# An encoder layer on one core: sums of weights and a product moved from GpSimd to VectorE, and the residual of the down projection added later

## The chip, the cores and the metric

The kernel runs on one core of a Trainium2 chip. A core has TensorE (PE in the rows), with its weight loads counted apart (PEld), VectorE (DVE), ScalarE (ACT), GpSimd (POOL) and SyncE (SP), which issues most DMAs. The metric is the device time of one execution in microseconds (us), the median of three runs; smaller is better.

## The reference

One layer of an encoder over 1024 + 256 tokens of width 1024: neighbourhood attention beside a short convolution, an output projection, a LayerNorm, then a gated feed-forward block. All is float32. The change touches the second half:

```python
x = layer_norm(DEEPNORM_ALPHA * x + mix, ln1_g, ln1_b)
h = dwconv3(x @ ffn_w_up + ffn_b_up, ffn_conv_w, ffn_conv_b)   # 1024 -> 5632
h_gate, h_val = jnp.split(h, 2, axis=-1)
f = (jax.nn.gelu(h_gate) * h_val) @ ffn_w_down + ffn_b_down    # 2816 -> 1024
return layer_norm(DEEPNORM_ALPHA * x + f, ln2_g, ln2_b)
```

## The kernel before

Each large product is done by Strassen's scheme in Winograd's form: seven products of half-size blocks in place of eight, with sums of the blocks before and after. Each block is split in a high part (a cast on ScalarE) and a low part (source less high part, on VectorE, line 69), and one product is three passes: high by high, low by high, high by low.

**The up projection** (class `Sevens`, lines 81 to 154; loop of line 1150) handles 22 pairs of 128-column tiles of the up weights: tile i of the gate with tile i of the value. A pair has four weight blocks a11, a12, a21, a22 (128x512 each, tile `ur`) and seven products in the order 1, 2, 6, 7, 4, 5, 3. Four sums of weight blocks are needed for a pair, and GpSimd makes them: line 112 (tile `us`), 113, 127 and 129. A slot n of the loop issues product n (24 matmuls of 128x320), then the split of the weights of product n + 2 (high part `uh`, low part `ul`, three buffers each, so the cast waits until product n - 1 has been read), then the eviction of product n - 1 (VectorE adds from PSUM, line 154), then what was put at that slot. At a pair's first product, four slots ahead, stand lines 112 and 113 (`sums_a`). After a pair's last product come its two convolutions (ScalarE line 997, VectorE lines 1000 to 1007), GELU on ScalarE (line 1012), the product of gate and value on GpSimd (line 1013), and its store (line 1014). Products of pairs 0 and 1 are interleaved, and beside them VectorE makes the seven forms of the activations (`xh`, `xl`).

**The down projection** (line 1374) runs seven products in the order 1, 7, 5, 6, 4, 2, 3, each of 11 steps; a step q is 15 matmuls of 128x512 (five token tiles t by three passes) into five of eight PSUM banks, and `dn_next` prepares the operands (`wd`, `fd`, `hr`) of a step some steps ahead. A product of the next kind starts on three free banks and then takes the first banks of the product before it, so these must be evicted by then. `at_step(q, f)` runs f after step q's matmuls are issued. The residual rows (x after the first LayerNorm, scaled by `gr` and shifted by `br`, lines 1214 and 1215) are loaded and scaled that way. Block c11 of product 1 is added by VectorE to the residual that already lies in `y` (line 1239), after ScalarE has copied the same bank into c12 (line 1237).

Each engine runs its instructions in the order in which the program issues them, so a waiting instruction holds up all that stands behind it on its engine.

Of the kernel before, what the change touches and what calls it, by code (L numbers as in the profile page):

```python
# [13 lines left out]
ALU = mybir.AluOpType  # L14
# [4 lines left out]
D = 1024  # L19
# [5 lines left out]
FFT = 22  # L25
# [14 lines left out]
def encoder_kernel(ctx: ExitStack, tc: tile.TileContext, a: dict, y_prompt, y_sample):  # L40
    nc = tc.nc

    def pool(name, side="left", bufs=1, space=None):
        kw = {} if space is None else {"space": space}
        if space is None:
            kw["side"] = side
        return tc.alloc_tile_pool(name=name, bufs=bufs, reuse_waits="tile", **kw)
# [23 lines left out]
    def split2(hi, lo, src):  # L71
        nc.scalar.copy(hi, src)  # L72
        diff(lo, src, hi.bitcast(F32))
# [7 lines left out]
    class Sevens:  # L81


        def __init__(self, seq, st, xops, uw, src, raw_tile, sum_tile, c_tile):
            self.seq, self.st, self.xops, self.uw, self.src = seq, st, xops, uw, src
            self.raw_tile, self.sum_tile, self.c_tile = raw_tile, sum_tile, c_tile
            self.pos = {ip: n for n, ip in enumerate(seq)}
            self.pairs = 1 + max(i for i, _ in seq)
            self.raws, self.sums, self.wops, self.slots, self.c, self.later = {}, {}, {}, {}, ({}, {}), {}
            self.done = set()  # L90
# [17 lines left out]
        def sums_a(self, i):  # L108
            if i < self.pairs:
                a11, a12, a21, a22 = self.blocks(i)  # L110
                self.sums[i] = self.sum_tile(i)
                nc.gpsimd.tensor_tensor(self.sums[i], a21, a22, ALU.add)  # L112
                nc.gpsimd.tensor_tensor(a21, a11, a21, ALU.subtract)

        def weights(self, n):
            if n >= len(self.seq) or n in self.done:
                return
            self.done.add(n)
            i, p = self.seq[n]
            a11, a12, a21, a22 = self.blocks(i)  # L120
            src = {1: a11, 2: a12, 6: a11, 7: a21, 4: a22, 5: self.sums.get(i), 3: a22}[p]
            wh, wl = self.wops[n] = [self.uw.tile([P, 512], F32R, tag=tag, name=tag, bufs=3) for tag in ("uh", "ul")]
            split2(wh, wl, src)
            if p == 1:
                if i not in self.sums:
                    self.sums_a(i)
                nc.gpsimd.tensor_tensor(a11, self.sums[i], a11, ALU.subtract)  # L127
            if p == 4:
                nc.gpsimd.tensor_tensor(a22, a12, a11, ALU.subtract)  # L129
                self.load(i + 2, 0)  # L130
            if p == 3:
                self.load(i + 2, 1)
# [29 lines left out]
    uw = pool("uw")  # L162
# [9 lines left out]
    def pair_of(p, pl):  # L172
        return [p.tile([P, 4, HALF], F32R, name=f"x{part}{pl}") for part in "hl"]

    xops = {p: pair_of(xqa, p) for p in (3, 2, 6)}
# [5 lines left out]
    def up_tile(tag, dt=F32):  # L181
        return up.tile([P, T], dt, tag=tag, name=tag, bufs={"c0": 2, "c1": 1, "o": 3, "wr": 2}[tag])
# [5 lines left out]
    def xblock(k, h):  # L188
        return xr[k][:, h * HALF:(h + 1) * HALF].rearrange("p (t c) -> p t c", c=P)
# [24 lines left out]
    def v_mm(ps, t, k):  # L214
# [8 lines left out]
    seq = [(i, p) for i in range(NPAIR) for p in ORDER]  # L223
    st = []
    pr7 = Sevens(seq, st, xops, uw, lambda i, g: a["w_in"][TILES[i][g]],
                 lambda i, g: uw.tile([P, 1024], F32, tag=f"ur{g}", name="ur", bufs=2),
                 lambda i: uw.tile([P, 512], F32, tag="us", name="us"),
                 lambda i, g: up_tile(f"c{g}"))

    v_dram = dram.tile([NT, P, 512], F32, name="v_dram")  # L230
    ps = {t: pa.tile([P, 512], F32, tag="pa", name="ps_v") for t in range(8)}
# [161 lines left out]
    for p, n in ((7, 0), (4, 1), (5, 2)):  # L393
        for k in range(4):
            src = {7: xblock(k, 0), 4: xblock(k + 4, 0), 5: xblock(k, 1)}[p]
# [417 lines left out]
    def bank():  # L813
        return cc.tile([P, 512], F32, tag="cc", name="ps_ch")
# [39 lines left out]
    st = [pool("st0", bufs=2, space=PSUM)]  # L854
# [7 lines left out]
    x1_dram = dram.tile([NT, P, D], F32, name="x1_dram")  # L862
# [45 lines left out]
    xops = {}  # L908
# [15 lines left out]
    for t, half in [(0, 0), (1, 0), (0, 1), (1, 1)] + [(t, half) for t in range(2, NT) for half in range(2)]:  # L924
# [4 lines left out]
        if t < 2 and half == 0:  # L929
            ps = early[t]  # L930
        else:
            ps = big.tile([P, 512], F32, tag="big", name="ps_o")
# [39 lines left out]
    uw = pool("uw")  # L972
    seq = [(i, p) for p in ORDER for i in range(2)] + [(i, p) for i in range(2, FFT) for p in ORDER]
# [9 lines left out]
            return last_c  # L983
        return (uw, up)[g].tile([P, T], F32, tag="c", name="c", bufs=2)

    up7 = Sevens(seq, st, xops, uw, lambda i, g: a["w_up"][i + g * FFT], raw_tile, sum_tile, c_tile)
    pos, NS = up7.pos, len(seq)
    c1, c2 = up7.c
    at_slot, run_slot = up7.at_slot, up7.run_slot
# [20 lines left out]

    def gated(i, o, u):
        nc.scalar.activation(o, o, AF.Gelu_apprx_tanh)  # L1012
        nc.gpsimd.tensor_tensor(o, o, u, ALU.mult)  # L1013
        nc.sync.dma_start(out=h_dram[i], in_=o)

    def value_conv(i, e):
# [18 lines left out]
    for i in range(2, FFT):  # L1035
        at_slot(pos[i, 3], lambda i=i: value_conv(i, pos[i, 3] + 1))
        at_slot(pos[i, 1] - 4, lambda i=i: sums_a(i))
# [31 lines left out]
    a11, hraws, wraws, hs, ws, ahead = {}, {}, {}, {}, {}, [0, 0]  # L1069
# [143 lines left out]
    def residual(dst, c):
        nc.vector.tensor_tensor(dst, dst, gr[:, c], ALU.mult)
        nc.vector.tensor_tensor(dst, dst, br[:, c], ALU.add)

    def add(dst, p, q):
        nc.vector.tensor_tensor(dst, p, q, ALU.add)  # L1218

    def add_sum(t, half, q):  # L1220

        cs = (L, R)[half]
        if t < HT - 1 or t >= HT:
            nc.vector.tensor_tensor_reduce(out=ys[t][:, cs], in0=ys[t][:, cs], in1=q, scale=1.0, scalar=0.0,
                                           op0=ALU.add, op1=ALU.add, accum_out=ss[t][:, 6 + half:7 + half])
        else:
            add(ys[t][:, cs], ys[t][:, cs], q)
            nc.vector.bn_stats(stats[t][:, half, :], ys[t][:, cs])
# [5 lines left out]
    def dn_evict(p, t, ps):  # L1234
        (c11, c12), (c21, c22) = ((ys[u][:, L], ys[u][:, R]) for u in (t, t + HT))
        if p in (1, 7, 5):
            nc.scalar.copy({1: c12, 7: c21, 5: c22}[p], ps)
        if p == 1:
            add(c11, c11, ps)
        if p == 6:  # L1240
            add(c12, c12, ps)
        if p == 4:
            add_sum(t + HT, 0, ps)
        if p in (2, 3):
            add_sum(t, int(p == 3), ps)
# [4 lines left out]
    def at_step(n, f):  # L1250
        beside.setdefault(n, []).append(f)
# [9 lines left out]
        nc.vector.scalar_tensor_tensor(br, br, ALPHA, rest["bd"], ALU.mult, ALU.add)  # L1261

    def left_in(t):
        nc.sync.dma_start(out=ys[t][:, L], in_=x1_dram[t][:, L])

    def right_in(t):
        rest[t] = dnraw[:, 0:3, :].rearrange("p a b -> p (a b)")[:, t * 512:(t + 1) * 512]
        nc.sync.dma_start(out=rest[t], in_=x1_dram[t][:, R])

    def row_in(t):  # L1270
        rest[t] = z_tile("yr")
        nc.sync.dma_start(out=rest[t], in_=x1_dram[t])

    def sums(t, part):
        (c11, c12), (c21, c22) = ((ys[u][:, L], ys[u][:, R]) for u in (t, t + HT))
        if part == 0:
            add(c21, c21, c12)
            add(c12, c12, c22)
        elif part == 1:
            add(c22, c22, c21)  # L1280
            add(c21, c21, rest[t + HT][:, L])
            add_sum(t + HT, 1, rest[t + HT][:, R])
        else:
            add(c12, c12, rest[t])
# [11 lines left out]
            store(t, slice(0, D))  # L1296

    at_step(0, rows_in)
    at_step(4, rows_scaled)
    at_step(40, lambda: (row_load(g2, "ln2_g"), row_load(b2, "ln2_b")))  # L1300
    for t in range(HT):
        u = t + HT
        for n, f in ((2 + t, lambda t=t: left_in(t)), (6 + t, lambda t=t: residual(ys[t][:, L], L)),
                     (12 + 2 * t, lambda u=u: row_in(u)), (16 + 2 * t, lambda u=u: residual(rest[u], slice(0, D))),
                     (26 + 2 * t, lambda t=t: right_in(t)), (30 + 2 * t, lambda t=t: residual(rest[t], R)),
                     (44 + 2 * t, lambda t=t: sums(t, 0)), (45 + 2 * t, lambda t=t: sums(t, 1)),
                     (56 + 2 * t, lambda t=t: sums(t, 2)),
                     ((55, 58, 61, 66, 69)[t], lambda u=u: second_norm(u, 0)),
                     ((57, 60, 63, 68, 70)[t], lambda u=u: second_norm(u, 1))):
            at_step(n, f)  # L1310
# [63 lines left out]
    for n, p in enumerate(DORDER):  # L1374
        ps = [banks[(5 * n + t + 4) % 8] for t in range(HT)]
# [131 lines left out]
```

## Time and profile before

| | |
|---|---|
| median of 3 runs | 1706.35 us (1704.37 to 1706.86) |
| profiled execution | 1705.61 us, of which the span of the profile is 1703.8 us |
| PE busy | 1654.1 us (97%) |
| PEld busy | 1534.1 us (90%) |
| DVE busy | 1299.6 us (76%) |
| ACT busy | 688.9 us (40%) |
| POOL busy | 485.6 us (28%) |
| up projection, about | 852 to 1421 us of the span |
| down projection, about | 1421 to 1692 us of the span |

Busy is the time in which an engine has an instruction running; matmuls overlap one another, so the busy share of PE says that it has work, not that it runs at its peak. An instruction that is held while it runs (here on VectorE) counts as busy for that time. Times in the rows are from the start of the span.

### The profile page before, as it was taken

To read this page: it belongs to the slowest core of one execution; us is meant where nothing else is said; L and a number is where in the kernel's file an instruction comes from. 1 tells how busy PE (TensorE), PEld (TensorE's weight loads), DVE (VectorE), ACT (ScalarE), POOL (GpSimd) and SP (SyncE) were. 2 spreads that over 40 slices of the span, in tenths; PEclk is the share of its full clock that TensorE was granted. 3 is DMA by queue.
4 is the path that set the end of the run, shared out by engine and by line. 5 is a ranking of instruction groups with operands and counts; after the bars stand their busy time and mean duration, and the time that the engine had idled before them with its cause. 6 is when DMAs were issued, how large, how long until landed. Compare 5 with 4: busy or idle time off the path is not lost.

```text
span 1703.8 us, 26121 instructions
## 1 busy us (share of the span) xinstructions
PE 1654.1 (97%) x9907; PEld 1534.1 (90%) x9915; DVE 1299.6 (76%) x2003; ACT 688.9 (40%) x1117; POOL 485.6 (28%) x423
## 2 busy tenths in 40 slices
PE   9999999999999998999999999999999999999997
PEld 7999999999997887777888899999999998788885
DVE  7567777877766776864689888888888888884886
ACT  4433344434445775323354333333333334332254
POOL 1221221222125672600012233333233232001145
PEclk9999999999999999999999999999999999999999
DMA  6277543677777551432401121122122117967753
GB/s 226 87 232 252 184 161 118 229 256 279 261 270 243 190 172 69 143 136 74 156 18 54 68 81 57 65 81 71 58 75 81 53 44 254 343 221 216 226 182 136
DMA packets 85196, 260.87 MB, mean 153 GB/s; under 512 B 9168, under 2 KB 16080, under 8 KB 85072
## 3 DMA queue, kind: packets, MB, share of 16 engines
q1 hardware_dynamic: 71392, 206.26, 34.9%
q0 software_dynamic: 11376, 44.57, 8.3%
q10 hardware_dynamic: 2304, 8.39, 1.4%
q8 instruction: 78, 1.28, 0.3%
q14 instruction: 46, 0.38, 0.1%
HBM read 171.10 MB, written 88.08 MB: 152 GB/s over the span
## 4 chain that ended last, share of the span: by engine, by line
PE 50%; DVE 9%; DMA 4%; issue 3%; ACT 2%; POOL 1%; SPq 0%; ACTq 0%; POOLq 0%; DVEq 0%
PE ps_x L57 26%; PE ps_dn L57 12%; PE ps_o L57 4%; PE ps_ch L591 3%; PE o_ps L57 2%; DVE ul L69 2%; PE s_ps L57 1%; PE t_ps L648 1%; DMA y<-x_dram 1%; DVE o L1000 1%; DMA ga<-sg_dram 1%; DVE ml L69 1%; DVE xl L69 1%; DVE c L154 1%; PE ps_ch L57 1%
## 5 line engine op out<-in xcount | busy, mean ns | idle before, releaser
L57 PE MATMUL ps_x<-xh,ul 128*128 128x320 f32 x2240 | 695.6, 311 | 8.0 <-DVE ul L69 7.5
L57 PE MATMUL ps_x<-xh,uh 128*128 128x320 f32 x2240 | 693.2, 309 | 1.1 <-ACT yb L899 0.7
L57 PE MATMUL ps_x<-xl,uh 128*128 128x320 f32 x2240 | 693.2, 309 | 0.4 <-DVE xl L69 0.3
L57 PEld LDWEIGHTS ps_x<-xh,ul 128*128 128x128 f32 x2240 | 422.1, 188 | 14.4 <-DVE ul L69 14.4
L57 PEld LDWEIGHTS ps_x<-xh,uh 128*128 128x128 f32 x2240 | 422.2, 188 | 1.8 <-ACT yb L899 1.1
L57 PEld LDWEIGHTS ps_x<-xl,uh 128*128 128x128 f32 x2240 | 422.2, 188 | 1.2 <-DVE xl L69 1.1
L69 DVE TENSOR_TENSOR ul<-ur,uh 128x512 fp32r<-128x512 f32 x240 | 203.8, 850 | 96.4 <-ACT uh L72 96.4
L57 PE MATMUL ps_dn<-wd,fd 128*128 128x512 f32 x1155 | 265.6, 392 | 6.6 <-DVE y L1218 3.6
L57 PEld LDWEIGHTS ps_dn<-wd,fd 128*128 128x128 f32 x1155 | 218.3, 189 | 53.6 <-DVE y L1218 4.0
L72 ACT CAST uh<-ur 128x512 fp32r<-128x512 f32 x240 | 147.0, 615 | 230.9 <-PE ps_x L57 182.2
L154 DVE TENSOR_TENSOR c<-ps_x,c 128x640 f32<-128x640 f32 x275 | 220.6, 813 | 1.1 <-PE ps_x L57 0.9
L129 POOL TENSOR_TENSOR ur<-ur 128x512 f32<-128x512 f32 x40 | 56.5, 1413 | 516.2 <-DVE ul L69 516.2
L69 DVE TENSOR_TENSOR ul<-us,uh 128x512 fp32r<-128x512 f32 x38 | 72.0, 1894 | 44.1 <-ACT uh L72 44.1
L997 ACT ACTIVATE o<-c,vec 128x1280 f32<-128x1280 f32 x43 | 62.5, 1458 | 78.5 <-DVE c L154 78.5
L1013 POOL TENSOR_TENSOR o<-o 128x1280 f32<-128x1280 f32 x22 | 65.4, 2975 | 92.7 <-ACT o L1012 80.0
L1000 DVE SCALAR_TENSOR_TENSOR o<-c,vec,o 128x1023 f32<-128x1023 f32 x86 | 89.4, 1040 | 1.6 <-ACT o L997 1.6
L1001 DVE SCALAR_TENSOR_TENSOR o<-c,vec,o 128x1023 f32<-128x1023 f32 x86 | 77.9, 905 | 3.0
L635 POOL TENSOR_TENSOR sp<-sp,stat 128x384 f32<-128x384 f32 (+1 forms) x80 | 59.5, 746 | 68.3 <-DVE stat L634 45.3
L112 POOL TENSOR_TENSOR us<-ur 128x512 f32<-128x512 f32 x38 | 50.9, 1340 | 91.6 <-DVE ul L69 47.9
L1012 ACT ACTIVATE o<-o 128x1280 f32<-128x1280 f32 x22 | 28.0, 1274 | 119.9 <-DVE o L1007 119.9
L1098 POOL DMA_DIRECT2D wd<-wd_dram x55 | 29.7, 539 | 160.6 <-PE ps_dn L57 144.4
L127 POOL TENSOR_TENSOR ur<-us,ur 128x512 f32<-128x512 f32 x38 | 49.6, 1304 | 83.6 <-DVE ul L69 83.5
(232 smaller groups left out, 2443.6 us busy)
## 6 DMA issues: line engine op xcount, KB each, us to landing
wd_dram<-wd SPq DMA_DIRECT2D x55, 512.0 KB, 3.3
wd<-wd_dram POOLq DMA_DIRECT2D x55, 512.0 KB, 4.5
ur<-in_w_up SPq DMA_DIRECT2D x44, 512.0 KB, 3.5
ur<-in_w_in SPq DMA_DIRECT2D x36, 512.0 KB, 4.4
qk_dram<-o SPq DMA_DIRECT2D x48, 320.0 KB, 5.5
h_dram<-o SPq DMA_DIRECT2D x22, 640.0 KB, 2.9
hr<-h_dram SPq DMA_DIRECT2D x33, 320.0 KB, 4.2
sg_dram<-c SPq DMA_DIRECT2D x16, 640.0 KB, 4.2
```

The lines of the kernel that those rows point to most:

```text
L57: nc.tensor.matmul(out, lhsT=l, rhs=r, start=(first and i == 0), stop=(last and i == n - 1))
L69: nc.vector.tensor_tensor(dst, p, q, ALU.subtract)
L72: nc.scalar.copy(hi, src)
L112: nc.gpsimd.tensor_tensor(self.sums[i], a21, a22, ALU.add)
L129: nc.gpsimd.tensor_tensor(a22, a12, a11, ALU.subtract)
L154: nc.vector.tensor_tensor(d, ps, q, ALU.add)
L591: nc.tensor.matmul(ps[:, :cn], lhsT=l, rhs=r, start=(i == 0), stop=(i == len(ops) - 1))
L635: nc.gpsimd.tensor_tensor(sp[:, :nk], sp[:, :nk], st[:, 2:3].to_broadcast([P, nk]), ALU.mult)
L997: nc.scalar.activation(o, c, AF.Identity, bias=beff[:, f:f + 1], scale=cw[1][:, f:f + 1])
L1000: nc.vector.scalar_tensor_tensor(o[:, s + 1:s + n], c[:, s:s + n - 1], w0, o[:, s + 1:s + n], ALU.mult, ALU.add)
L1001: nc.vector.scalar_tensor_tensor(o[:, s:s + n - 1], c[:, s + 1:s + n], w2, o[:, s:s + n - 1], ALU.mult, ALU.add)
L1013: nc.gpsimd.tensor_tensor(o, o, u, ALU.mult)
```

## The change

The class `Sevens` gets the engine of its sums as an argument: GpSimd as before for the input projection, VectorE for the up projection. The product of gate and value goes to VectorE as well. In the down projection the eviction of product 1 is two copies by ScalarE; the left residual is loaded into a buffer of its own (`yl`, from the ring of five `z` buffers), scaled there and added to `y` by VectorE at steps of the second product. The steps at which rows are loaded and scaled move back: the scaling of `gr` and `br` from step 4 to 10, the left rows from steps 2 to 10 to steps 9 to 22, the rows of the lower half from steps 12 to 24 to steps 20 to 32, the right rows from steps 26 to 38 to steps 29 to 41.

```diff
@@ class Sevens
-                nc.gpsimd.tensor_tensor(self.sums[i], a21, a22, ALU.add)
-                nc.gpsimd.tensor_tensor(a21, a11, a21, ALU.subtract)
+                self.eng.tensor_tensor(self.sums[i], a21, a22, ALU.add)
+                self.eng.tensor_tensor(a21, a11, a21, ALU.subtract)
...
-                nc.gpsimd.tensor_tensor(a11, self.sums[i], a11, ALU.subtract)
+                self.eng.tensor_tensor(a11, self.sums[i], a11, ALU.subtract)
             if p == 4:
-                nc.gpsimd.tensor_tensor(a22, a12, a11, ALU.subtract)
+                self.eng.tensor_tensor(a22, a12, a11, ALU.subtract)
@@ pr7 = Sevens(...)
-                 lambda i, g: up_tile(f"c{g}"))
+                 lambda i, g: up_tile(f"c{g}"), nc.gpsimd)
@@ up7 = Sevens(...)
-    up7 = Sevens(seq, st, xops, uw, lambda i, g: a["w_up"][i + g * FFT], raw_tile, sum_tile, c_tile)
+    up7 = Sevens(seq, st, xops, uw, lambda i, g: a["w_up"][i + g * FFT], raw_tile, sum_tile, c_tile, nc.vector)
@@ def gated
-        nc.gpsimd.tensor_tensor(o, o, u, ALU.mult)
+        nc.vector.tensor_tensor(o, o, u, ALU.mult)
@@ def dn_evict
         if p == 1:
-            add(c11, c11, ps)
+            nc.scalar.copy(c11, ps)
@@ def left_in
-        nc.sync.dma_start(out=ys[t][:, L], in_=x1_dram[t][:, L])
+        rest["l", t] = z_tile("yl")[:, L]
+        nc.sync.dma_start(out=rest["l", t], in_=x1_dram[t][:, L])
@@ at_step
-    at_step(4, rows_scaled)
+    at_step(10, rows_scaled)
...
-        for n, f in ((2 + t, lambda t=t: left_in(t)), (6 + t, lambda t=t: residual(ys[t][:, L], L)),
...
+        for n, f in ((9 + 2 * t, lambda t=t: left_in(t)), (13 + 2 * t, lambda t=t: residual(rest["l", t], L)),
+                     (14 + 2 * t, lambda t=t: add(ys[t][:, L], ys[t][:, L], rest["l", t])),
```

On VectorE, where the first pairs are worked on (`xl_9303` is the low part of the last form of the activations, `ur` here the weights of pair 2 and `us` their sum):

```order
 L69 TENSOR_TENSOR ul<-ur,uh 128x512
 L154 TENSOR_TENSOR c<-ps_x_9272,c 128x640
+L112 TENSOR_TENSOR us<-ur 128x512
+L113 TENSOR_TENSOR ur<-ur 128x512
 L69 TENSOR_TENSOR xl_9303<-yb_7971,xh_9302 128x640 x2
 L69 TENSOR_TENSOR ul<-ur,uh 128x512
 L154 TENSOR_TENSOR c<-ps_x_9308,c 128x640 x2
 L69 TENSOR_TENSOR ul<-ur,uh 128x512
+L127 TENSOR_TENSOR ur<-us,ur 128x512
```

Two sums now stand between an eviction and the low parts of the activations, and a third behind the low part of pair 2's first product.

On VectorE, at the border of two pairs in the steady part (`o` is the gate after its convolution, the product with it is line 1013):

```order
 L1006 TENSOR_SCALAR o_9441<-o_9441,t_443 128x2
 L1007 TENSOR_SCALAR o_9441<-o_9441,nw_444 128x2
+L1013 TENSOR_TENSOR o_9441<-o_9441 128x1280
 L69 TENSOR_TENSOR ul<-us,uh 128x512
 L154 TENSOR_TENSOR c<-ps_x_9770,c 128x640
+L112 TENSOR_TENSOR us<-ur 128x512
+L113 TENSOR_TENSOR ur<-ur 128x512
 L69 TENSOR_TENSOR ul<-ur,uh 128x512
 L154 TENSOR_TENSOR c<-ps_x_9810,c 128x640
 L69 TENSOR_TENSOR ul<-ur,uh 128x512
+L127 TENSOR_TENSOR ur<-us,ur 128x512
```

The product of line 1013, which takes the result of GELU, stands directly behind the last step of the convolution and ahead of the low part of the pair's product 5 (`us`).

On VectorE, at the change from the up to the down projection, behind the convolution of the last pair (`wd` and `fd` are operands of the down projection's step 4):

```order
 L1006 TENSOR_SCALAR o<-o,t_443 128x2
 L1007 TENSOR_SCALAR o<-o,nw_444 128x2
+L1013 TENSOR_TENSOR o<-o 128x1280
 L69 TENSOR_TENSOR wd<-hr,wd 128x512
 L69 TENSOR_TENSOR fd<-a_4_14232,fd 128x640
```

The last product of gate and value stands ahead of the operands of step 4.

## Rows read from the trace of the kernel before

**Rows 1.** Stretches: length, busy us by engine (instructions), clock, DMA share, GB/s

```profile
900.00:945.00 45.00, 38.70 (x253) 37.65 (x252) 41.08 (x51) 15.69 (x18) 16.55 (x9) 0.97 0.23 77
988.00:1013.00 25.00, 24.97 (x171) 24.70 (x170) 21.58 (x27) 8.69 (x11) 8.54 (x6) 1.00 0.20 69
1431.00:1442.00 11.00, 9.47 (x41) 7.47 (x41) 10.35 (x15) 6.80 (x11) 3.56 (x2) 1.00 0.63 193
1464.00:1471.00 7.00, 5.17 (x12) 4.11 (x13) 6.97 (x11) 3.11 (x6) 0.53 (x1) 0.52 0.95 334
1471.00:1500.00 29.00, 29.00 (x129) 23.95 (x129) 23.59 (x30) 8.66 (x14) 1.58 (x3) 1.00 0.85 285
```

**Rows 2.** Waits of PE: who waits for whom, us in total, times, longest

```profile
PE ps_x L57 <- DVE ul L69: 7.5, 6, 2.8
PE ps_dn L57 <- DVE y L1218: 3.6, 1, 3.6
```

**Rows 3.** Timeline, borders of pairs: start, us, engine, instruction [idle before <-releaser]

```profile
964.60 0.42 PE L57 MATMUL ps_x<-xh,ul 128*128 128x320 f32 x1 [1.09 <-DVE ul L69]
...
1059.11 0.22 DVE L1007 TENSOR_SCALAR o<-o,nw 128x2 f32<-128x2 f32 x1
1059.43 1.27 ACT L1012 ACTIVATE o<-o 128x1280 f32<-128x1280 f32 x1 [5.40 <-DVE o L1007]
1060.78 2.97 POOL L1013 TENSOR_TENSOR o<-o 128x1280 f32<-128x1280 f32 x1 [2.64 <-ACT o L1012]
1061.24 3.05 DVE L69 TENSOR_TENSOR ul<-us,uh 128x512 fp32r<-128x512 f32 x1 [1.91 <-ACT uh L72]
1064.01 0.31 PE L57 MATMUL ps_x<-xl,uh 128*128 128x320 f32 x1
1064.35 0.41 PE L57 MATMUL ps_x<-xh,ul 128*128 128x320 f32 x1
```

**Rows 4.** Groups by form, DVE from 965 to 1364 us: count, busy, mean ns, idle before

```profile
L69 DVE TENSOR_TENSOR ul<-ur,uh 128x512 fp32r<-128x512 f32 x96 | 91.3, 951 | 20.8 <-ACT uh L72 20.8
L69 DVE TENSOR_TENSOR ul<-us,uh 128x512 fp32r<-128x512 f32 x16 | 48.8, 3051 | 30.8 <-ACT uh L72 30.8
```

**Rows 5.** Groups by form, DVE from 850 us on

```profile
L1214 DVE TENSOR_TENSOR y<-y,dnraw 128x512 f32<-128x512 f32 x5 | 3.4, 689 | 1.0 <-DMA y<-x_dram 1.0
```

**Rows 6.** Timeline, first pairs of the up projection

```profile
892.97 1.35 ACT L72 CAST xh<-yb 128x640 fp32r<-128x640 f32 x2 [4.10 <-POOL ur L129]
...
902.15 1.55 DVE L69 TENSOR_TENSOR xl<-yb,xh 128x640 fp32r<-128x640 f32 x2
...
905.21 1.30 POOL L112 TENSOR_TENSOR us<-ur 128x512 f32<-128x512 f32 x1 [12.27 <-DMA ur<-in_w_up]
905.69 1.37 DVE L69 TENSOR_TENSOR ul<-ur,uh 128x512 fp32r<-128x512 f32 x1
...
940.02 2.98 DVE L69 TENSOR_TENSOR ul<-ur,uh 128x512 fp32r<-128x512 f32 x1 [1.91 <-ACT uh L72]
```

**Rows 7.** Timeline, change from the up to the down projection

```profile
1432.65 0.50 PE L57 MATMUL ps_dn<-wd,fd 128*128 128x512 f32 x1 [1.53 <-DVE fd L69]
1434.00 1.28 ACT L1012 ACTIVATE o<-o 128x1280 f32<-128x1280 f32 x1 [6.28 <-DVE o L1007]
1434.42 0.82 DVE L69 TENSOR_TENSOR fd<-a,fd 128x640 fp32r<-128x640 f32 x1
1435.41 2.96 POOL L1013 TENSOR_TENSOR o<-o 128x1280 f32<-128x1280 f32 x1 [22.34 <-ACT o L1012]
```

**Rows 8.** Timeline, end of the down projection's first product

```profile
1462.70 0.72 ACT L1116 CAST fd<-hr 128x640 fp32r<-128x640 f32 x1 [2.38 <-DVE hr L69]
1463.34 2.53 ACT L1237 COPY y<-ps_dn 128x512 f32<-128x512 f32 x5
1465.10 3.07 DVE L1218 TENSOR_TENSOR y<-y,ps_dn 128x512 f32<-128x512 f32 x5
1465.83 0.80 PE L57 MATMUL ps_dn<-wd,fd 128*128 128x512 f32 x1 [3.62 <-DVE y L1218]
```

More of the change, by code (lines that the diff above doesn't have):

```diff
@@ L81, in encoder_kernel, with __init__ @@
     class Sevens:
-        def __init__(self, seq, st, xops, uw, src, raw_tile, sum_tile, c_tile):
+        def __init__(self, seq, st, xops, uw, src, raw_tile, sum_tile, c_tile, eng):
             self.seq, self.st, self.xops, self.uw, self.src = seq, st, xops, uw, src
-            self.raw_tile, self.sum_tile, self.c_tile = raw_tile, sum_tile, c_tile
+            self.raw_tile, self.sum_tile, self.c_tile, self.eng = raw_tile, sum_tile, c_tile, eng
             self.pos = {ip: n for n, ip in enumerate(seq)}
@@ L1298, in encoder_kernel @@
     at_step(0, rows_in)
-    at_step(4, rows_scaled)
-    at_step(40, lambda: (row_load(g2, "ln2_g"), row_load(b2, "ln2_b")))
+    at_step(10, rows_scaled)
+    at_step(42, lambda: (row_load(g2, "ln2_g"), row_load(b2, "ln2_b")))
     for t in range(HT):
         u = t + HT
-        for n, f in ((2 + t, lambda t=t: left_in(t)), (6 + t, lambda t=t: residual(ys[t][:, L], L)),
-                     (12 + 2 * t, lambda u=u: row_in(u)), (16 + 2 * t, lambda u=u: residual(rest[u], slice(0, D))),
-                     (26 + 2 * t, lambda t=t: right_in(t)), (30 + 2 * t, lambda t=t: residual(rest[t], R)),
+        for n, f in ((9 + 2 * t, lambda t=t: left_in(t)), (13 + 2 * t, lambda t=t: residual(rest["l", t], L)),
+                     (14 + 2 * t, lambda t=t: add(ys[t][:, L], ys[t][:, L], rest["l", t])),
+                     (20 + 2 * t, lambda u=u: row_in(u)), (24 + 2 * t, lambda u=u: residual(rest[u], slice(0, D))),
+                     (29 + 2 * t, lambda t=t: right_in(t)), (33 + 2 * t, lambda t=t: residual(rest[t], R)),
                      (44 + 2 * t, lambda t=t: sums(t, 0)), (45 + 2 * t, lambda t=t: sums(t, 1)),
```

## The prediction

> **What bounds the kernel now.** I read the busy time by stretches first, then what PE waited for, then the timeline at the places where it waited. In the steady part of the up projection PE is busy 24.97 of 25 us, DVE 21.58, at full clock [rows 1]: PE sets the pace, and there a faster or slower DVE changes nothing until DVE has over some 3 us more to do per pair. So only the places count at which PE stands still. In the two stages that the change touches there are three of any size: 7.5 us for the low parts `ul` and 3.6 us for the evictions by line 1218 [rows 2], and 1.5 us for an operand `fd` [rows 7]. The timeline puts them in four places: the first pairs (a stretch in which DVE is busy 41.08 of 45 us and PE 38.70 [rows 1]), the border of each pair [rows 3], the change to the down projection [rows 7], and the end of the down projection's first product [rows 8].
>
> The row to understand first is `ul<-us` at a pair's border. It takes 3.05 us, where the same form takes 0.69 alone. It starts while POOL's line 1013 runs (1060.78 to 1063.75) and ends 0.54 us after that [rows 3]: DVE is held for as long as POOL works. On the mean, `ul<-us` takes 3.05 us and `ul<-ur` 0.951 [rows 4], against 0.689 for a 128x512 operation of two SBUF operands beside which POOL has nothing [rows 5].
>
> **Steady part.** Per pair DVE gets four 128x512 sums, 4 x 0.69 = 2.76 us, and the 128x1280 product. That one is not in the trace for DVE; from 0.689 for 512 columns [rows 5] and 0.82 for 640 [rows 7], 0.131 per 128 columns, I take 0.82 + 5 x 0.131 = 1.48 us. The far ends are 2.5 x 0.82 = 2.05 and POOL's own 2.97 [rows 3]; nothing excludes a price a little lower. Added: 4.24 us. Removed, as no POOL work is left there: 3.05 - 0.69 = 2.4 and 6 x (0.951 - 0.69) = 1.6, together 4.0 us. DVE's work per pair stays, 21.6 + 0.2 of 24.9 us, so PE goes on setting the pace. What changes is the order at the border. The convolution ends at 1059.3, GELU runs to 1060.7, the product on DVE would run from 1060.75 to 1062.25 and `ul<-us` to 1062.95. PE wants it at 1064.01 + 0.15 = 1064.16 and got it at 1064.35 [rows 3]. The DVE product waits for GELU, and behind it stand `ul<-us` and an eviction; in that time DVE idled before too (1.91 us for the cast, which itself stood behind GELU [rows 3]), so this wait costs nothing. The two sums behind it (1.4 us) cover what POOL's sums cost the next `ul` by holding it. So the small loss of each border goes. There are 19 of them from 963 to 1413 us: the first loses 1.25 (PE idle 1.09 in its row), one 0.5, and seventeen 0.15 to 0.2, as from 1064.01 to 1064.35 less the 0.147 us of a matmul [rows 3]; the sum is 4.9 us. **Term: -4.9 us** (0 if DVE is late by as much for another reason).
>
> *A page on the other side.* The Trainium skill, Perfetto Trace Analysis, Optimizing Scalar/DVE Operations, says that GpSimd and VectorE share an SBUF read port, so that moving operations between the two might not help. The trace agrees as to the port [rows 3, 4]. By that sentence the up projection's terms would be nothing; this is the second rival below.
>
> **First pairs.** DVE's queue decides here up to the first product of pair 3, whose `ul` PE takes at once when it ends at 940.02 + 2.98 = 943.0 [rows 6]. I sum what happens to that queue from 902.15 to 943.0. Seven instructions are held by POOL in it, from the `ul` at 905.69 (1.37 us) to the one at 940.02 (2.98) [rows 6]; with the four between they take 13.9 us, and alone 3 x 0.69 + 4 convolution steps of 3.5 together, so 8.3 us go. Six sums come, 6 x 0.69 = 4.1, and two products, 3.0. A new wait comes: lines 112 and 113 of pair 2 now stand on DVE ahead of `xl` at 902.15, but the weights that they read land only at 905.21, as POOL's wait shows [rows 6]; DVE stands 3.1 us, with the last low parts of the activations behind it, and PE behind these for 1.5 to 2 us. GELU's wait takes the place of the 1.91 us before 940.02, -0.5. Together +1.4 us. Against it the queue arrives earlier: the cast `xh` at 892.97 waited for POOL's line 129 [rows 6], which on DVE ends 0.9 us sooner (0.6 us of delay by three sums ahead of the last LayerNorm included). **Term: +0.5 us**, from -1.5 (sums at 0.60 apart, not 0.69) to +4 (PE's stand at 905 not made good, or the clock of the next paragraph but one).
>
> **Change of projections.** PE waits at 1432.65 for the fourth `fd`, made behind the last pair's convolution [rows 7]; nothing in that chain moves. GELU then runs from 1434.00 to 1435.28 [rows 7]. In the changed order DVE waits for it and does the product, to 1436.8, and only then the `wd` and `fd` of step 4, which it made at 1433.8 to 1435.2 before [rows 7]. They are done at 1436.8 + 0.69 + 0.82 - 0.1 = 1438.2. PE takes 15 matmuls of 29/129 = 0.225 us for a step [rows 1], so it comes to step 4 at 1432.65 + 3.4 = 1436.0, and wants the low part 0.2 later: a stand of 2.0 us. Before, step 5 waited 0.24 for a `wd` held by POOL's product (1435.41, [rows 7]), which goes. The store behind the product leaves SP 1.5 us sooner, and the loads behind it too; no one waits for these. **Term: +1.7 us** (0 to +5.1, if the clock falls as well).
>
> **End of the first product of the down projection.** PE waited 3.62 us for line 1218 at 1465.83. The five adds stood behind ten scalings of residual rows, and ScalarE's copies of the same banks, at 1463.34, behind a cast that waited 2.38 us for DVE's `hr` [rows 8], which stood behind the same scalings: ten of 0.69 and 1.0 us of waiting for rows [rows 5], 7.9 us. In the changed kernel no residual is on DVE by then and the banks are released by ScalarE alone, in ten copies of some 0.5 us (2.53 for five [rows 8]). The first bank is done 12 matmuls before the product's end and wanted 9 after it, 21 x 0.225 = 4.7 us, for two copies; the second the next 3. So nothing is late: -3.6 us. Behind the stand PE ran at half its clock: 12 matmuls in 5.17 us from 1465.83 on, 0.43 each, with a granted clock of 0.52, which is the 1.2 GHz level [rows 1]; 12 x (0.43 - 0.225) = 2.5 us go with it. **Term: -6.1 us** (-3.0 if the first stands half). What is moved: the scalings and five adds, 15 x 0.69 = 10.4 us of DVE, lie beside steps 13 to 22, and the next rows' beside steps 24 to 32. DVE has 23.59 busy of 29 us at 1471 to 1500, much of it the scalings of the next rows, which leave this stretch [rows 1]; so it has room. The loads of the rows move with them, out of a stretch with the DMAs near full, and wait for nothing.
>
> **The sum** against the profiled execution of 1705.61 us: -4.9 + 0.5 + 1.7 - 6.1 = -8.8, so 1696.8. That execution lies 0.74 under the median of 1706.35, from which 1697.5 follows.
>
> **Rivals.** *The clock falls at the new stand.* PE would stand 1.5 us at 1431 and 2.0 us at 1436. A stand of 3.6 cost the full clock [rows 1, 8], one of 1.5 did not (1.00 from 1431 to 1442 [rows 1]); two so near are between. Price: a stretch like that from 1464 to 1471, 7 us at 0.52, takes 3.4 us of PE's work, so 1701. The Trainium skill, TensorE: Matmul & The Clock Gate, What's actually happening, says that the gate follows how busy TensorE has been recently, which speaks for it; no run here shows this pair of stands. 25%.
> *The up projection gives nothing*: its gains at the borders come back as waits of DVE for GELU or for the weights. Then only -6.1 + 1.7 + 0.5 are left: 1702.5. Against it: 1.2 us of room at each border. 10%.
> *The banks stay late*, for ScalarE's casts before the copies wait for DVE in any case: -8.8 + 6.1, so 1703.6. Against it: 7.9 us less in front of them. 7%.
> *Slower: DVE becomes the bound of the up projection.* If its product of 128x1280 takes as long as POOL's 2.97, and the sums 1.3, the length of POOL's line 112 [rows 6], then 1.5 + 4 x 0.6 = 3.9 us come per pair on top of 21.8 and 1.35 of waiting for GELU, 27.1 against PE's 24.7: 2.4 x 19 = +45 us, 1743. It decides from 2.7 us for the product on, where `ul<-us` passes 1064.16; at 3.0 it costs 0.3 x 19, which with the rest makes no change, and with sums over 0.9 us it is slower. Against it stands that DVE's operations of this kind take 0.69 wherever POOL is idle. 6%.
> The forecast itself: 52%, with 1693 to 1700 as its own range, where the lower end is a kernel in which the first pairs keep the full clock.
>
> **Range and chances.** 1691 to 1704.5 holds the forecast and the first three rivals. 0.2%, 3.4 us, is about what a measurement of this kernel can tell from no change, so under 1702.9 is faster. Of the forecast 0.50 lies there, of the clock rival 0.20, half of the second and a third of the third, 0.07: 0.77. Slower takes its 0.06 and 0.03 for what I have not thought of, 0.09; 0.14 are left for the same.
>
> **What would show it.** `ul<-us` and `ul<-ur` at 0.69 us; line 1013 on DVE near 1.5 us, and no idle time of PE at the pairs' borders; DVE's busy time per pair near 21.8 of 24.7 us; a wait of DVE's line 112 for `in_w_up` of some 3 us near 901; PE waiting about 2 us for `fd` two steps into the down projection; no wait of PE at the end of its first product, and the clock at 1.00 behind it. Wrong it would be if DVE's product took over 2.7 us, if the 24.7 us per pair grew, or if a wait of PE for DVE appeared in steps 20 to 35, where the residual rows now lie.

## The result, and the profile after

| | before | after |
|---|---|---|
| median | 1705.36 us (1702.74 to 1706.86, 4 runs) | 1694.75 us (1694.19 to 1695.97, 4 runs) |
| ratio | | 0.9947, 95% interval 0.9935 to 0.9958 |
| profiled execution, its span | 1705.61, 1703.8 us | 1694.82, 1693.0 us |
| DVE, POOL busy | 1299.6, 485.6 us | 1290.2, 297.1 us |

The changed kernel is faster: the two medians lie 10.6 us apart, and the ratio on record is 9.0 us (7.2 to 11.1). 8.8 were forecast, and 1697.5 us against the 1694.75 measured. Where they come from is seen best by following TensorE: the start of one and the same matmul in both traces, and the difference.

| matmul | before | after | difference |
|---|---|---|---|
| first of product 0 of the up projection | 851.97 | 850.97 | -1.0 |
| first of product 14 | 910.87 | 913.99 | +3.1 |
| first of product 26 | 963.06 | 962.23 | -0.8 |
| first of the down projection | 1420.51 | 1413.68 | -6.8 |
| first of its step 4 | 1435.96 | 1428.42 | -7.5 |
| first of its step 6 | 1443.01 | 1439.00 | -4.0 |
| first of its step 22 | 1503.77 | 1493.40 | -10.4 |
| last | 1692.25 | 1681.42 | -10.8 |

The first row can't be put down to the change. In the traces of all the runs below product 0 starts between 850.07 and 851.81 us, and at 850.22 us in one whose kernel is the kernel before up to the last pair.

Stretches of the changed kernel (columns as in [rows 1]):

```profile
900.00:945.00 45.00, 39.11 (x247) 38.06 (x247) 38.51 (x57) 15.15 (x18) 0.00 (x0) 0.95 0.21 77
988.00:1013.00 25.00, 25.00 (x173) 25.00 (x172) 21.94 (x34) 9.04 (x12) 0.00 (x0) 1.00 0.25 86
1430.64:1435.20 4.56, 4.56 (x13) 3.60 (x14) 3.17 (x5) 1.20 (x3) 0.00 (x0) 0.65 1.02 395
1452.00:1464.00 12.00, 12.00 (x55) 9.94 (x54) 7.59 (x11) 7.71 (x14) 2.11 (x4) 1.00 0.89 305
1471.00:1500.00 29.00, 29.00 (x130) 24.02 (x129) 24.73 (x36) 12.52 (x21) 0.00 (x0) 1.00 0.80 270
```

The third row is new: 4.56 us in which TensorE has a granted clock of 0.65, where before it kept 1.00 [rows 1]. The fourth takes the place of the stretch at 0.52 [rows 1]: TensorE goes through the end of the down projection's first product without a pause. TensorE's waits in the two stages:

```profile
PE ps_x L57 <- DVE ul L69: 3.9, 3, 2.2
PE ps_dn L57 <- DVE fd L69: 2.6, 2, 1.8
PE ps_x L57 <- DVE xl L69: 2.4, 2, 2.2
```

Of the 7.5 us for `ul` 3.9 are left, the 3.6 us for line 1218 [rows 2] are gone, the wait for `fd` grew (one of 1.53 us before [rows 7]), and one of 2.2 us for `xl` came. A border of pairs, and VectorE's groups from 958 to 1358 us:

```profile
1056.35 0.22 DVE L1007 TENSOR_SCALAR o<-o,nw 128x2 f32<-128x2 f32 x1
1056.66 1.27 ACT L1012 ACTIVATE o<-o 128x1280 f32<-128x1280 f32 x1 [4.81 <-DVE o L1007]
1057.97 1.49 DVE L1013 TENSOR_TENSOR o<-o 128x1280 f32<-128x1280 f32 x1 [1.40 <-ACT o L1012]
1059.38 0.69 DVE L69 TENSOR_TENSOR ul<-us,uh 128x512 fp32r<-128x512 f32 x1
...
1061.83 0.31 PE L57 MATMUL ps_x<-xl,uh 128*128 128x320 f32 x1
1061.98 0.31 PE L57 MATMUL ps_x<-xh,ul 128*128 128x320 f32 x1
```

```profile
L69 DVE TENSOR_TENSOR ul<-ur,uh 128x512 fp32r<-128x512 f32 x97 | 66.5, 686 | 27.2 <-ACT uh L72 27.1
L1013 DVE TENSOR_TENSOR o<-o 128x1280 f32<-128x1280 f32 x17 | 25.4, 1493 | 24.1 <-ACT o L1012 24.1
L69 DVE TENSOR_TENSOR ul<-us,uh 128x512 fp32r<-128x512 f32 x17 | 11.6, 685 | 0.0
L112 DVE TENSOR_TENSOR us<-ur 128x512 f32<-128x512 f32 x17 | 11.6, 680 | 0.0
```

`ul<-us` fell from 3.05 to 0.69 us and ends 1.9 us before TensorE's pass needs it [rows 3, 4]. Here are the two places where something was lost, the first pairs and step 4 of the down projection:

```profile
904.12 0.69 DVE L112 TENSOR_TENSOR us<-ur 128x512 f32<-128x512 f32 x1 [2.79 <-DMA ur<-in_w_up]
905.46 1.55 DVE L69 TENSOR_TENSOR xl<-yb,xh 128x640 fp32r<-128x640 f32 x2
906.33 0.62 PE L57 MATMUL ps_x<-xl,uh 128*128 128x320 f32 x1 [2.23 <-DVE xl L69]
...
1427.76 1.49 DVE L1013 TENSOR_TENSOR o<-o 128x1280 f32<-128x1280 f32 x1 [1.40 <-ACT o L1012]
1429.17 0.69 DVE L69 TENSOR_TENSOR wd<-hr,wd 128x512 fp32r<-128x512 f32 x1
1429.28 0.32 SPq L1014 DMA_DIRECT2D h_dram<-o  x1
1429.77 0.82 DVE L69 TENSOR_TENSOR fd<-a,fd 128x640 fp32r<-128x640 f32 x1
1430.64 14.63 PE L57 MATMUL ps_dn<-wd,fd 128*128 128x512 f32 x56 [1.84 <-DVE fd L69]
```

### The profile page after: what moved, and what is told of

Same layout as the page of the kernel before. It is cut to its first block, busy times and chain, and to the rows that moved or that the text cites. A ratio compares the mean times of both kernels' runs of the same rounds, so it can differ in the third digit from the quotient of the medians.

```text
span 1693.0 us, 26079 instructions
## 1 busy us (share of the span) xinstructions
PE 1648.4 (97%) x9907; PEld 1533.0 (91%) x9915; DVE 1290.2 (76%) x2113; ACT 693.6 (41%) x1122; POOL 297.1 (18%) x313
## 5 line engine op out<-in xcount | busy, mean ns | idle before, releaser
L69 DVE TENSOR_TENSOR ul<-ur,uh 128x512 fp32r<-128x512 f32 x240 | 168.8, 704 | 102.6 <-ACT uh L72 102.5
L1001 DVE SCALAR_TENSOR_TENSOR o<-c,vec,o 128x1023 f32<-128x1023 f32 x86 | 76.0, 884 | 3.1
L1000 DVE SCALAR_TENSOR_TENSOR o<-c,vec,o 128x1023 f32<-128x1023 f32 x86 | 75.4, 877 | 1.6 <-ACT o L997 1.6
L591 PE MATMUL ps_ch<-yc,wh 128*128 128x512 f32 (+1 forms) x192 | 66.8, 385 | 3.6 <-DVE mc L595 1.8
L129 POOL TENSOR_TENSOR ur<-ur 128x512 f32<-128x512 f32 x18 | 26.5, 1473 | 248.4 <-DVE ul L69 248.4
L57 PE MATMUL ps_o<-woh,mh 128*128 128x512 f32 x160 | 65.9, 412 | 1.5 <-ACT woh L794 1.5
L57 PE MATMUL ps_o<-wol,mh 128*128 128x512 f32 x160 | 63.9, 399 | 0.9 <-DVE wol L795 0.9
L57 PE MATMUL ps_o<-woh,ml 128*128 128x512 f32 x160 | 63.2, 395 | 0.0
```

Source lines behind the costliest of these rows:

```text
L57: nc.tensor.matmul(out, lhsT=l, rhs=r, start=(first and i == 0), stop=(last and i == n - 1))
L69: nc.vector.tensor_tensor(dst, p, q, ALU.subtract)
L129: self.eng.tensor_tensor(a22, a12, a11, ALU.subtract)
L591: nc.tensor.matmul(ps[:, :cn], lhsT=l, rhs=r, start=(i == 0), stop=(i == len(ops) - 1))
L1000: nc.vector.scalar_tensor_tensor(o[:, s + 1:s + n], c[:, s:s + n - 1], w0, o[:, s + 1:s + n], ALU.mult, ALU.add)
L1001: nc.vector.scalar_tensor_tensor(o[:, s:s + n - 1], c[:, s + 1:s + n], w2, o[:, s:s + n - 1], ALU.mult, ALU.add)
```

## The experiments

The kernel before took 1703.87 us in the runs beside the first four told, 1705.13 beside the one with the sum made three times, 1703.99 beside the four after it, and 1704.06 beside the last three. The ratios are those on record against these runs; they can differ from the quotient of the two medians by 0.0005.

**Which part of the change does it.** Four kernels, each with a part of the diff shown above. First the up projection's part alone, the down projection as before:

```diff
-    up7 = Sevens(..., c_tile, nc.gpsimd)
+    up7 = Sevens(..., c_tile, nc.vector)
-        nc.gpsimd.tensor_tensor(o, o, u, ALU.mult)
+        nc.vector.tensor_tensor(o, o, u, ALU.mult)
```

> Only the up projection's part of the change (sums and product on VectorE); the down projection as before. Theory: the parts add up. In the trace of the changed kernel TensorE is 4.0 us ahead of the kernel before at step 5 of the down projection; here the stand of 3.6 us for the eviction adds and the half clock behind it come back, so about 4 us under the kernel before, 1701.4 (1699.5 to 1703.5). Rival: the gain at the borders of pairs counts only because the later stand is gone too, so no change here, within 1.5 us of the kernel before.

Measured: 1695.15 us (ratio 0.9948, 0.9934 to 0.9961), the whole change's time. The expectation failed: the stand at the end of the first product is gone though nothing of the down projection was changed.

The down projection's part alone:

> Only the down projection's part (two copies by ScalarE, residual later); sums and product on GpSimd as before. Theory: the stand at the end of the first product (3.6 us) and the half clock behind it (2.5 us) go, 6.1 to 6.4 us under the kernel before, 1699 (1697.5 to 1700.5), and no wait of TensorE there. Rival: GpSimd's last product still holds VectorE by 3 us near 1436, the copies come late, and half of the gain or more is missing: 1702 or above.

Measured: 1697.36 us (0.9964, 0.9952 to 0.9977), 6.5 us less, just under the expected range, and TensorE doesn't wait at the end of the first product. So each part removes that same stand, and the gains don't add: by the medians beside them 8.7 and 6.5 us alone, 9.0 to 10.6 together.

The sums on VectorE and the product on GpSimd, the down projection as changed (`nc.gpsimd.tensor_tensor(o, o, u, ALU.mult)` left as it was):

> The changed kernel, but with the product of gate and value on GpSimd again: of the up part only the sums are moved. Theory: the instruction held at a pair's border is the low part of product 5, held by the product on GpSimd, so it still takes about 3 us and the borders still lose 0.2 us each; the ul from the weights themselves fall to 0.69. The change of projections has no new stand. So the down part's gain with little else: 1699 (1697 to 1700.5). Rival: it is the sums on GpSimd that make VectorE late: the borders' loss goes, and the time is 1695 or below.

Measured: 1712.84 us (1.0052, 1.0040 to 1.0065), slower than before, which neither side expected. And the other way round, the product on VectorE and the sums on GpSimd (`up7 = Sevens(..., nc.gpsimd)`):

> The changed kernel, but with the sums of the up weights on GpSimd again: of the up part only the product is moved. Theory: the borders' loss goes entirely (the low part of product 5 at 0.69), TensorE needs 24.63 us per pair; the wait of VectorE for the weights of pair 2 and TensorE's stand near 904 go; the new stand two steps into the down projection stays. 1694.5 (1692.5 to 1696.5), the same as the changed kernel or a little faster. Rival: without moving the sums the other low parts stay stretched and TensorE still waits at the borders: 1698 or above.

Measured: 1690.67 us (0.9923, 0.9911 to 0.9936), 4.1 us faster than the whole change and 1.8 below the range of its theory, which had put the cost of the sums too low. With the down part in all of them, the sums cost 15.5 us (1697.36 to 1712.84) and the product gains 6.7 (to 1690.67). Why, is seen in 400 us of the steady part, by the count of matmuls (168 make a pair). Before:

```profile
1000.00:1400.00 400.00, 399.23 (x2696) 395.05 (x2694) 344.92 (x418) 139.73 (x178) 135.68 (x80) 1.00 0.19 67
```

The changed kernel:

```profile
1000.00:1400.00 400.00, 400.00 (x2729) 400.00 (x2728) 343.92 (x507) 142.45 (x178) 0.00 (x0) 1.00 0.20 67
```

The sums on VectorE, the product on GpSimd:

```profile
1000.00:1400.00 400.00, 390.31 (x2636) 386.37 (x2635) 342.67 (x471) 137.73 (x174) 45.65 (x16) 1.00 0.18 65
```

The product on VectorE, the sums on GpSimd:

```profile
1000.00:1400.00 400.00, 400.00 (x2730) 400.00 (x2729) 324.31 (x440) 144.91 (x179) 89.59 (x65) 1.00 0.19 67
```

TensorE's own pace is 24.64 us a pair, as the second and fourth have it. VectorE is busy 86% in all but the last, and yet the third is the slowest; busy time doesn't tell which engine sets the pace. The distance from one `ul<-us` to the next does. In the kernel before the next after the one at 1061.24 [rows 3] is

```profile
1086.18 3.05 DVE L69 TENSOR_TENSOR ul<-us,uh 128x512 fp32r<-128x512 f32 x1 [1.91 <-ACT uh L72]
```

and with the sums on VectorE and the product on GpSimd:

```profile
1064.80 0.22 DVE L1007 TENSOR_SCALAR o<-o,nw 128x2 f32<-128x2 f32 x1
1066.93 3.05 DVE L69 TENSOR_TENSOR ul<-us,uh 128x512 fp32r<-128x512 f32 x1 [1.91 <-ACT uh L72]
...
1078.87 0.69 DVE L69 TENSOR_TENSOR ul<-ur,uh 128x512 fp32r<-128x512 f32 x1 [1.36 <-ACT uh L72]
...
1090.69 1.27 ACT L1012 ACTIVATE o<-o 128x1280 f32<-128x1280 f32 x1 [6.04 <-DVE o L1007]
1091.86 0.60 ACT L72 CAST uh<-us 128x512 fp32r<-128x512 f32 x1
1092.50 3.05 DVE L69 TENSOR_TENSOR ul<-us,uh 128x512 fp32r<-128x512 f32 x1 [1.91 <-ACT uh L72]
```

That is 24.94 and 25.57 us. VectorE's row is gapless but for the waits of 1.36 and 1.91 us for ScalarE (1.30 and 1.91 in the kernel before), and ScalarE's convolution step and GELU, behind which those casts stand, wait for VectorE in turn. It is a closed chain of two engines, and its length was the pace already in the kernel before. Four sums add 4 x 0.69 = 2.76 us to it; without GpSimd's sums beside them three `ul` of 1.27, 1.04 and 1.33 us and a convolution step of 1.07 become 0.69, 0.69, 0.69 and 0.48, 2.2 us less; together +0.6, measured +0.63. Against the kernel with the down part alone TensorE takes 10.5 us more in the 18 pairs from product 28 on, and 3.9 more from product 0 to 28; these are nearly all of the 15.5. With the product on VectorE the stretch from L1007 to the end of `ul<-us` takes 3.72 us in place of 5.18, so the chain of the changed kernel is 25.57 - 1.46 = 24.1 us, 0.5 below TensorE's; without the sums it is 23.5. The test of this reckoning makes the first sum three times over:

```diff
-                self.eng.tensor_tensor(self.sums[i], a21, a22, ALU.add)
+                for _ in range(3 if self.eng is nc.vector else 1):
+                    self.eng.tensor_tensor(self.sums[i], a21, a22, ALU.add)
```

> The changed kernel, in which VectorE makes the first sum of each pair of the up projection (L112) three times over; the two added ones change nothing in the data. Theory: VectorE's row is a closed chain from one border to the next, with two waits for ScalarE in it that VectorE itself releases; it takes 25.57 us with the sums on VectorE and the product on GpSimd, and 1.46 us less, 24.1 us, in the changed kernel, against 24.64 us of TensorE. Two sums more, 0.60 to 0.72 us each, make it 25.3 to 25.5, so 0.7 to 0.9 us per pair in 17 to 19 pairs: 12 to 17 us, and 0 to 4 us in the first pairs: 1707 to 1716 us. Rival, the reckoning of the prediction: VectorE is busy 21.9 of 24.6 us per pair, so 1.4 us more still fit in, and only the first pairs pay: 1695 to 1699 us.

Measured: 1713.98 us (1.0050, 1.0036 to 1.0064). Its borders (line numbers one higher):

```profile
1043.42 0.68 DVE L69 TENSOR_TENSOR ul<-us,uh 128x512 fp32r<-128x512 f32 x1
1068.91 0.68 DVE L69 TENSOR_TENSOR ul<-us,uh 128x512 fp32r<-128x512 f32 x1
1094.40 0.69 DVE L69 TENSOR_TENSOR ul<-us,uh 128x512 fp32r<-128x512 f32 x1
```

25.49 us a pair, within the 25.3 to 25.5 that the chain gives; the rival, which goes by busy time, is out by 15 us. By TensorE's place 15.0 us of the difference from the changed kernel lie in the 18 pairs from product 28 on, 0.83 a pair, as the chain has it, and 5.0 ahead of product 28, where 0 to 4 were expected.

**The sums' other price, at 904 us.** In the changed kernel the two sums of pair 2 come one slot later:

```diff
-            at_slot(pos[i, 1] - 4, lambda i=i: sums_a(i))
+            at_slot(pos[i, 1] - (3 if i == 2 else 4), lambda i=i: sums_a(i))
```

> The changed kernel with one edit: the two sums of pair 2 that stood in slot 10 (L112, L113) come one slot later, behind the xl of that slot. Theory: all that the sums cost on VectorE lies at 904 to 909 us, where L112 waits 2.79 us for a transfer with the xl behind it, TensorE stands 2.2 us and then runs 3.4 us at half clock. Both go: 2.2 + 1.7 = 3.9 us, 1694.75 - 3.9 = 1690.8 us, the time of the kernel with the product alone on VectorE (1690.67). First rival: the sums cost by their time on VectorE, spread over the pairs, and the stand hides nothing else: within 1 us of 1694.75. Second rival: one slot later is too late for the next products, and the stand comes back there: 1694 to 1697.

Measured: 1691.76 us (0.9923, 0.9910 to 0.9937), 3.0 less where 3.9 were expected. The wait for the weights and TensorE's stand for `xl` are gone, and with the clock at 1.00 TensorE is 4.2 us earlier at product 14. But 2.7 of it are lost again by product 28, behind two stands of 1.0 and 1.2 us at 957 to 960 us with the clock at 0.72 after them, and 1.6 are gained at step 4, which the edit doesn't touch. There TensorE stands as long as in the changed kernel, as its row says:

```profile
1429.13 16.16 PE L57 MATMUL ps_dn<-wd,fd 128*128 128x512 f32 x70 [1.84 <-DVE fd L69]
```

yet the clock stays at 1.00, unlike that behind the two stands (stretches, columns as in [rows 1]):

```profile
1429.20:1433.80 4.60, 4.60 (x21) 3.79 (x21) 3.17 (x5) 1.27 (x3) 0.57 (x1) 1.00 1.01 366
960.50:966.50 6.00, 6.00 (x32) 6.00 (x32) 5.76 (x10) 0.62 (x1) 0.00 (x0) 0.72 0.54 191
```

So the place of the loss is shown; its size in this kernel is right only in the sum of things of which the theory named one. The others are falls of the clock that come and go from trace to trace (last section).

**The stand at step 4.** In the changed kernel the last pair's product goes behind the operands of step 4:

```diff
+        if i < FFT - 1:
+            times(i, o, u)
+        else:
+            held.append(lambda: times(i, o, u))
...
         if n > NS:
             dn_next()
+        if n == NS + 2:
+            held.pop()()
```

> The changed kernel with one edit: the product of the last pair's gate (1.49 us, L1013) and its store come behind the wd and fd of step 4 of the down projection. Theory: the stand of 2.0 us at 1428.4 us and the 3.4 us at half clock behind it are there only because that product stands ahead of wd and fd on VectorE: 2.0 + 1.7 = 3.7 us less, 1694.75 - 3.7 = 1691.0 us. Rival: the store that follows the product also lets out the loads behind it in the sync queue, these come later, and the stand moves to step 5 to 7 or to the end of the first product: 1693 to 1696 us.

Measured: 1691.68 us (0.9923, 0.9910 to 0.9937), as the theory has it (3.1 of 3.7 us). TensorE's row goes on from step 3 without a wait:

```profile
1415.80 7.42 PE L57 MATMUL ps_dn<-wd,fd 128*128 128x512 f32 x32
1424.03 16.16 PE L57 MATMUL ps_dn<-wd,fd 128*128 128x512 f32 x70 [0.81 <-DVE fd L69]
```

The same with the sums on GpSimd:

> Sums on GpSimd as before, product on VectorE, the last pair's product behind the wd and fd of step 4, down projection as changed. Theory: the two gains add, since they lie 500 us apart: 1690.67 - 3.7 = 1687.0 us. Rival: the stand moves to a later step of the down projection: 1689 to 1692 us.

Measured: 1687.73 us (0.9901, 0.9888 to 0.9915); the two gains add.

**What made the stand at the end of the first product.** The kernel before with the product on VectorE and nothing else:

> The kernel before with the product of the gate on VectorE and nothing else (sums on GpSimd, the down projection as before). Theory: the stand at the end of the down projection's first product hung on the product on GpSimd: it held the store and with it the loads of the left halves behind it in the sync queue. With the product on VectorE it is gone without the other part of the change: 1690.67 + 0.5 = 1691.2 us, within 1 us. Rival: the new order of the residuals and the copies on ScalarE are what removes it, and it comes back here: 1690.67 + 5.5 to 6.1 = 1696.2 to 1696.8 us.

Measured: 1690.98 us (0.9921, 0.9908 to 0.9935). The rest of the change adds nothing to that one word. And with only the last pair's product on VectorE:

```diff
-        nc.gpsimd.tensor_tensor(o, o, u, ALU.mult)
+        (nc.vector if i == FFT - 1 else nc.gpsimd).tensor_tensor(o, o, u, ALU.mult)
```

> The kernel before with only the last pair's product on VectorE; the 20 others and the sums on GpSimd, the down projection as before. Theory: the borders keep their price, step 4 of the down projection costs 2.8 us more as in the other kernels with that product on VectorE, and the stand at the end of the first product (5.1 to 5.7 us) goes, since VectorE's wd is no longer held and the store leaves earlier: 1703.99 + 2.8 - 5.4 = 1701.4 us. Rival: the stand comes from the order of the residuals and not from that one product: 1703.99 + 2.8 = 1706.8 us.

Measured: 1701.31 us (0.9984, 0.9975 to 0.9993), as expected (GpSimd keeps 21 products, not 20). The rows of before at the change of projections:

```profile
1435.81 3.10 DVE L69 TENSOR_TENSOR wd<-hr,wd 128x512 fp32r<-128x512 f32 x1 [0.58 <-ACT wd L1114]
1438.39 0.32 SPq L1014 DMA_DIRECT2D h_dram<-o  x1
1451.73 0.69 DVE L1214 TENSOR_TENSOR y<-y,dnraw 128x512 f32<-128x512 f32 x1 [0.30 <-DMA y<-x_dram]
```

and of this kernel:

```profile
1432.88 1.27 ACT L1012 ACTIVATE o<-o 128x1280 f32<-128x1280 f32 x1 [6.29 <-DVE o L1007]
1434.19 1.49 DVE L1013 TENSOR_TENSOR o<-o 128x1280 f32<-128x1280 f32 x1 [1.40 <-ACT o L1012]
1435.71 0.32 SPq L1014 DMA_DIRECT2D h_dram<-o  x1
1448.90 0.68 DVE L1214 TENSOR_TENSOR y<-y,dnraw 128x512 f32<-128x512 f32 x1
1461.43 3.07 DVE L1218 TENSOR_TENSOR y<-y,ps_dn 128x512 f32<-128x512 f32 x5
```

GpSimd's product held a `wd` for 2.4 us, and let the store out 4.4 us after GELU's start (1434.00 [rows 7]) in place of 2.8, with the loads behind it in the sync queue; VectorE then waits four times for such loads in before, 2.0 us together, and not once here. TensorE comes to step 11 at 1460.01 in before and at 1462.41 here, by its loss at step 4; the adds of line 1218 begin 5.1 us after that moment in before [rows 8] and 1.0 us ahead of it here. So VectorE was late by the hold and by the waits together, and the old order of the residuals makes no stand of that size without them. No run takes the hold without the waits, so the share of each is not shown.

Is it gone only because TensorE loses at step 4? The product alone on VectorE, with the hold of the last one as above:

> The kernel before with the product of the gate on VectorE, the last pair's product behind the wd and fd of step 4, sums on GpSimd and the down projection as before. Theory: the residuals in the first product do no harm by themselves, so the gain of 3.7 us at step 4 stays: 1690.98 - 3.7 = 1687.3 us, within 1 us of 1687.73, and the new order of the residuals adds nothing. Rival: in the kernel with the product alone the residuals only kept up because TensorE lost 3.7 us at step 4; without that loss they are late again at the end of the first product, and 2 to 6 us come back: 1689.5 to 1693 us.

Measured: 1687.59 us (0.9904, 0.9891 to 0.9918), as the theory has it and level with 1687.73: with this one word and this hold, the other edits of the change are worth nothing. The rival left a trace: the adds begin 1.5 us after the first matmul of step 11 in place of 0.3 ahead of it, and that step takes 0.3 us more. This is the best version, 7.2 us below the changed kernel.

The down part alone, with the copies into c11 on VectorE in place of ScalarE:

```diff
-            nc.scalar.copy(c11, ps)
+            nc.vector.tensor_copy(c11, ps)
```

> The kernel before with the new order of the residuals in the down projection, but the five banks of the first product copied out by VectorE and not by ScalarE; sums and product on GpSimd. Theory: the order is what counts: without the ten residual operations (6.9 us) in front, VectorE reaches the five copies (some 3 us) in time, and the time is that of the kernel with the whole down part (1697.36), within 1 us. Rival: VectorE in its row is what made the banks late, and the copies must leave it: 1700 to 1704 us.

Measured: 1698.40 us (0.9967, 0.9955 to 0.9979), at the edge of the theory's 1 us: the order is worth 5.7 us, the engine of the copies at most 1.

## Why the prediction was right, and where it was not

| term | predicted | by TensorE's place in the traces |
|---|---|---|
| ahead of product 0 | 0 | -1.0 |
| first pairs, product 0 to 26 | +0.5 | +0.2 |
| borders of pairs, to 1413 us | -4.9 | -6.0 |
| change of projections, to step 6 | +1.7 | +2.8 |
| end of the first product, to step 22 | -6.1 | -6.4 |
| later | 0 | -0.5 |
| sum (terms rounded) | -8.8 | -10.8 |

*Borders.* The mechanism held in every row named: `ul<-us` at 0.69, the product at 1.49 (1.48 forecast), no idle time of TensorE behind the first border (0.64 us there, 1.09 before [rows 3]). The size came out low, since 0.15 to 0.2 us was taken for each of seventeen borders and TensorE gained 0.31 us at each (24.95 to 24.64 us a pair): the matmul behind the one at 1064.35 [rows 3] was late by another 0.1. What failed is a sentence on the way: "PE sets the pace", with some 3 us of room for VectorE. The chain VectorE and ScalarE set the pace before, and in the changed kernel the room is 0.5 us. The rival in which VectorE becomes the bound put the turning point at 2.7 us for the product; by the chain it lies at 1.49 + 0.5 = 2.0 us.

*First pairs.* The wait of line 112 came as forecast (2.79 us for 3.1, at 904 us) and TensorE stood 2.2 us for `xl`. The clock fell behind that stand, which the term left to its upper end: counted from product 0, TensorE is 4.1 us behind at product 14. But VectorE's queue decided, as the prediction says. The matmul of product 21 that waits for the last of the `ul` in its sum starts thus, before and after:

```profile
943.05 0.63 PE L57 MATMUL ps_x<-xh,ul 128*128 128x320 f32 x1 [2.46 <-DVE ul L69]
943.28 0.42 PE L57 MATMUL ps_x<-xh,ul 128*128 128x320 f32 x1 [1.06 <-DVE ul L69]
```

It is 0.2 us later, or 1.2 counted from product 0, where 0.5 were forecast. From there to product 26 the changed kernel makes up 1.1 us. The granted clock was 0.51 from 942 to 949 us before and 0.61 from 943.0 to 947.2 after, both the lower level for a part of the stretch, and for longer before. The sum had no such gain, and the last section shows that it can't be put down to the change.

*Change of projections.* The stand of 2.0 us came where it was put. The first rival, that the clock falls behind it, came true as well, with 1.7 us in place of 3.4; the main forecast left it out. So the total comes out close with errors of opposite sign, this one (+1.1) and the borders (-1.1). That is luck.

*End of the first product.* The size is right, but the text gives the gain to the change of the down projection. The runs show two causes that are each enough: without GpSimd's last product the old order of the residuals is in time (1690.98 against 1690.67 us), and with the new order GpSimd's product does no harm. The step that failed is "the banks stood behind ten scalings", told as the whole cause; the rows of the held `wd` and of the late store stand 25 us ahead of it. The prediction saw both in the paragraph before and left them out here: of the loads behind that store it says "no one waits for these", and VectorE waited 2.0 us for them, of which the sum has 1.0 as a wait for rows.

*The port rule.* `ul<-us` goes from 3.05 to 0.69 us when GpSimd's operation beside it goes. This agrees with the Trainium skill, SBUF — State Buffer, Who interferes with whom, by which the port pair that VectorE and GpSimd share is an exclusive lock. The sentence of the Trainium skill, Perfetto Trace Analysis, Optimizing Scalar/DVE Operations, that was weighed in the prediction, that moving work between these two might not help, is right for the sums (+15.5 us) and wrong for the product (-6.7, and -13.0 where the old down part's stand goes with it). The rows tell them apart: the sums held VectorE for 2.2 us of a pair and are 2.76 of work there; the product held it for 2.4 behind a wait of 1.91, and is 1.49 of work behind one of 1.40.

## What to carry to other kernels

Before room is read off a busy share, follow one engine's row from a point to the same point of the next round, with its waits, and see whether those are released by its own earlier work; such a round trip is as hard a bound as a full engine. Test the parts of a change apart, since two can cure the same wait and one can hide the cost of another: here one operation moved gave all of the gain, and the sums that went with it cost 4 us. Before a difference at one place of two traces is put down to a change, see whether two kernels that are alike up to there differ as much. When an operation enters the row of a busy engine at a change of stages, look at what stands behind it there, and put it behind what the next stage wants first.

## What was not expected of the hardware

A stand of TensorE of the same length was not always followed by the lower clock: after the stand at step 4 (1.84 us in the row) the granted clock fell in the changed kernel (0.65 over 4.56 us) and stayed at 1.00 in the kernel with pair 2's sums later. Matmuls of 128x320 start every 0.147 us at the clock of 1.00 and every 0.267 after such a fall, those of 128x512 every 0.227 and 0.427, so not quite at half the rate.

The instructions alone don't decide it. The kernel before and the one with only the last pair's product on VectorE are alike up to the last pair, and in both TensorE stood 2.8 us and then 2.5 us, between 932 and 943 us. In the kernel before the clock was then 0.51 from 942 to 949 us, and 1.00 from 963.4 to 966.8. In the other it was 1.00 from 941 to 948 us, and 0.50, the 1.2 GHz level, from 963.4 to 966.8, behind stands of 1.0 and 2.4 us. So 1 to 3 us at one place of a single trace can be the clock and not the change, and the terms by TensorE's place are no surer than that. What decides between the two cases these runs don't settle.
